# Two-layer streaming trunk on one core: squares behind two z products, token blocks in pairs, z between halves of q, k, v, swapped queries copied on ScalarE

## The chip, the core and the metric

The kernel runs on one core of a Trainium2 chip. The core has TensorE (matrix products; PE in the profile, its weight loads PEld), VectorE (DVE), ScalarE (ACT), GpSimd (POOL) and SyncE (SP, which here issues nearly all the DMAs). Each engine runs its own list of instructions in order and waits on semaphores for the others. The metric is the device time of one execution in microseconds; the time of a kernel is the median of its runs.

## The reference

The input x has 2048 tokens of 1024 channels. Layer A is a gated pooling mixer, layer B stick-breaking attention; both end in a gated embedding add.

```python
def pool_mixer(h, w_in, w_group, scale, w_out):
    u, z = jnp.split(h @ w_in, 2, axis=-1)
    ...
    mixed = jnp.einsum('bsgc,gcd->bsgd', pooled, w_group).reshape(B, S, D_MODEL) * scale
    return (mixed * jax.nn.silu(z)) @ w_out

def reference(x, p, ...):
    for i in range(DEPTH):                     # 2 layers
        if i < N_A:
            h = rms_norm(x, a_norm[i])
            x = x + pool_mixer(h, a_w_in[i], a_w_group[i], a_scale[i], a_w_out[i])
        else:
            kv_in = rms_norm(x, kv_norm)
            k_all, v_all = jnp.split(kv_in @ w_kv, 2, axis=-1)
            k_sh = rms_norm(split_heads(k_all), k_norm)
            v_sh = split_heads(v_all)
            h = rms_norm(x, b_norm[j])
            q, z = jnp.split(h @ b_w_in[j], 2, axis=-1)
            q = rms_norm(split_heads(q), b_q_norm[j])
            o = stick_breaking_attention(q, k_sh, v_sh)   # 16 heads of 64
            x = x + (o * jax.nn.silu(z)) @ b_w_out[j]
        x = x + (p[i] @ ple_w[i]) * jax.nn.sigmoid(x @ ple_gate_w[i])
    return x
```

All of it is float32. The kernel keeps that precision by splitting an operand into a high and a low part, so that one product takes three matmuls (high x high, high x low, low x high).

## The kernel before

**Tiles.** Tokens are cut into four chunks of 512 (`s` or `c`). Activations are held as 8 tiles of 128 channels x 512 tokens, each a pair (high, low): `xp` is the input, `mp` the mixer's result, `x1` and `x2` the stream after the mixer and after layer A. Weights come in units of 512 KB, the buffers `wpair`, nine in all (`UNITS`). A product of z, of the gate or of an output takes a unit for two tiles of input channels; a unit of q, k or v (`plan_wide`) holds one tile of input channels (`kt` 0 to 7) for 512 output columns. The list `plan` sets the order in which units are loaded. `take` hands them out, `give_back` releases one behind its last matmul and lets the next load start.

A unit that is seen for the first time is loaded raw (`wraw`, 256 KB) and split by ScalarE (L176) and VectorE (L177); most are also stored split (`once`), and later chunks load the 512 KB from there. The q, k, v weights come in two halves of eight heads (`b` 0 and 1). The second half is stored in chunk 1 only, so chunks 0 and 1 both split it.

**The stream.** All dense work is one generator, `stream`. For each chunk `first_part` runs the mixer, the output product, the gate and the embedding product, then z of layer B (`gate_z`) and q, k, v of half 0; `second_part` runs q, k, v of half 1. In chunk 3 z stands behind q, k, v of half 0. Behind the last chunk comes `post`, the end of layer B for each chunk.

**q, k and v.** `kvq` computes one of them for one half: four token blocks `j` of 128 tokens, each over eight `kt`: 32 steps of three matmuls (`psd<-wpair,x` in the profile). The list `STEPS` is the order of the steps: token block 0, then 1, then 2 and 3 overlapped. A unit is given back behind its step with `j == 3`. A finished block goes from PSUM through ScalarE: `keyed` normalises rows of q and k per head, `valued` takes v. The rows of q and k are transposed (`finish`, queued in `lag`) at fixed steps of the following block, those of (1, 2), (1, 6), (2, 2), (3, 1). The token norm `r2` is made once per chunk, by whoever needs it first.

**Attention.** It starts when q, k, v of half 0 of chunk 0 are done. From there on TensorE's order is fixed by program order: `front` (logits of 128 queries with 512 keys), `turn` (transposes of the weights), `gather` (products with the values), and between them `fill` takes a set number of steps of the stream, more in early chunks and fewer in late ones. For each head, `load_q` fetches the query tile `qa` (two parts of 64 rows) and `qb`, the same with its parts swapped; both multiply the key tile.

**The start.** Before the attention `dense` takes banks of three tags and a scheduler may move instructions. At the very start (`boot`, `mixer_first`) the weights of the pooled branch are folded, and the first chunk's tokens are squared on ScalarE (L417) and summed by TensorE with narrow 128x1 matmuls (`square_first`), between the matmuls of the second z product. `norm_first` makes of it the norm that the mixer waits for.

Of the kernel before, what the change touches and what calls it, by code (L numbers as in the profile page):

```python
# [19 lines left out]
KT = D // P  # L20
NH = 16
HD = 64
W5 = 512
WB = 256
NSUB = S // W5
# [7 lines left out]
def f(ap):  # L33
    return ap.bitcast(F32)
# [3 lines left out]
def trunk_kernel(ctx, tc, x, p, a_norm, wu_t, wz_a, w_group, a_scale, a_w_out, kv_norm, w_kv,  # L38
                 k_norm, b_norm, b_w_q, b_w_z, b_q_norm, b_w_out, ple_a, ple_b, gate_a, gate_b, out):
    nc = tc.nc  # L40
    V, A, G = nc.vector, nc.scalar, nc.gpsimd
# [202 lines left out]
    for s in range(NSUB):  # L244
        for g in (3, 2, 1, 0):
            if s == 0:
                plan_group(g)
            plan_block("za", wz_a, g, g_a, True)
            plan_block("wf", None, g)
        for b in range(4):  # L250
            plan_block("ao", a_w_out, b, keep=True, order=PAIRS[::-1])
        for b in range(4):
            plan_block("ag", gate_a, b, keep=True)
            plan_block("al", ple_a, b, keep=True, order=PAIRS[:1])
        if s + 1 == NSUB:
            plan_kvq(s, 0)
        for b in range(4):
            plan_block("zb", b_w_z, b, g_b, True)
        if s + 1 < NSUB:
            plan_kvq(s, 0)  # L260
        plan_kvq(s, 1)
        if s == 0:
            first_chunk = len(plan)
# [149 lines left out]
    def square_first(i):  # L413
# [4 lines left out]
        for j in range(4):  # L418
            T.matmul(chunk[0]["sums"][:, 0, j : j + 1], sq[:, j * P : (j + 1) * P], ones,
                     start=(i + j == 0), stop=(i == KT - 1 and j == 3))  # L420

    def norm_first():
        chunk[0]["rb1"] = bcast(rooted(chunk[0].pop("sums"), "x"), "x")

    def warm():
        ps = bank("pso", "warm")
# [86 lines left out]
    def mixer_first():  # L513
        ck = chunk[0]
        ck["m"] = {}
        us = take(4)
        pss = [dense(), dense()]
        yield from product(pss[0], us, ck["x"], 0, 0)
        hooks = {3 * i: [lambda i=i: square_first(i)] for i in range(KT)}
        yield from hooked(product(pss[1], us, ck["x"], P, 1), hooks)  # L520
        while later:
            later.pop(0)()
        us = take(4)
        zs = []
        hooks = {8: [norm_first], 9: [lambda: zs.extend(silu(ps, ck["rb1"]) for ps in pss)]}
        for k in range(2):
            ps = dense()
            yield from hooked(product(ps, us, ck["x"], k * P, k), {} if k else hooks)
            pooled(0, 6 + k, ps, zs[k])
        state["boot"] = state["hold"] = False  # L530
        fold_load(2)
        while later:
            later.pop(0)()
# [91 lines left out]

    lag = []

    STEPS = [(j, kt) for j in range(2) for kt in range(KT)]
    STEPS += [(2, 0), (2, 1), (2, 2), (2, 3), (3, 0), (2, 4), (3, 1), (2, 5), (3, 2), (2, 6), (3, 3), (2, 7)]
    STEPS += [(3, kt) for kt in range(4, KT)]  # L630

    def kvq(s, kind, b):
        ck = chunk[s]
        us = take(KT)
        banks = {}
        for j, kt in STEPS:
            tk = slice(j * P, (j + 1) * P)
            if kt == 0:
                banks[j] = dense()
            u = us[kt][0]  # L640
            for xh, wh in ((0, 0), (1, 0), (0, 1)):
                T.matmul(banks[j], ck["x2"][kt][:, xh, tk], u[:, wh, 0], start=(kt == 0 and xh == wh),
                         stop=(kt == KT - 1 and wh == 1))
                if j == 3 and wh:
                    give_back()
                yield
            if lag and (j, kt) in ((1, 2), (1, 6), (2, 2), (3, 1)):
                lag.pop(0)()
            if kt < KT - 1:
                continue  # L650
            if "r2" not in ck:
                ck["r2"] = token_norm(ck["acc2"], "y")
            rj = ck["r2"][:, j : j + 1]
            (valued if kind == "v" else keyed)(s, kind, b, j, banks.pop(j), rj)

    def valued(s, kind, b, j, ps, rj):
        vr = row("vr")
# [124 lines left out]
    def first_part(s):  # L782
        ck = chunk[s]
        yield from mixer(s)
        x1 = yield from out_steps(ck["m"], lambda o: x[o * P : (o + 1) * P, s * W5 : (s + 1) * W5])
        ple = load_ple(0, s)
        yield from gate_steps(x1, ple, put_x2(s))
        ck["side"] = prep(s + 1) if s + 1 < NSUB else iter(())
        if s + 1 < NSUB:
            yield from every(gate_z(s), 48, ck["side"])  # L790
        for kind in "qkv":
            yield from every(kvq(s, kind, 0), 48, ck["side"])
        after(60, lambda: marks.add((s, 0)))
        if s + 1 == NSUB:
            yield from gate_z(s)

    def second_part(s):
        ck = chunk[s]
# [55 lines left out]
    def load_q(c, h):  # L854
        qa, qb = qryt("qa"), qryt("qb")
        nc.sync.dma_start(out=f(qa), in_=qd[c][h].rearrange("l d n -> (l d) n"))
        for l in range(2):
            nc.sync.dma_start(out=f(qb)[(1 - l) * HD : (2 - l) * HD], in_=qd[c][h][l])
        return qa, qb

    def load_k(kc, h):
        kk = keyt("kk")
# [17 lines left out]
    def front(st, j):  # L880
# [1 line left out]
        r0 = W5 - w  # L882
        ps = bank("psl", "psl")
        qs = slice(j * P, (j + 1) * P)
        (qa, qb), kk = st["q"], st["k"]
# [202 lines left out]
```

## Time and profile before

| | |
|---|---|
| Runs (us) | 2770.01, 2779.59, 2778.19 |
| Median (us) | 2778.19 |
| Profiled execution, its own time (us) | 2769.64 |
| Its span (us) | 2767.9 |
| Mean granted TensorE clock | 0.991 |
| DMA | 684.27 MB, mean 247 GB/s |

Stages of the profiled execution, by the matmuls on TensorE: the first z products and squares 13 to 50 us; the q, k, v stages 289 to 445 us (chunk 0, both halves, the start of the attention at 384 among them), 711 to 893 (chunk 1), 1215 to 1428 (chunk 2), 1751 to 1871 and 1948 to 2074 (chunk 3, with z between). A busy TensorE is not one at its peak, as ends of matmuls are modelled; what counts here is idle time between them and the granted clock.

### The profile page before, as it was taken

The page shows a single profiled execution, that of the slowest core. Times are in us where ns is not written, and L with a number is a line of the kernel's source. Part 1 is how long each engine was busy: PE and PEld are TensorE (multiplying, and loading weights), DVE is VectorE, ACT ScalarE, POOL GpSimd, SP SyncE. Part 2 cuts the span into 40 slices and gives each one's busy share as a digit, 9 for nine tenths or more (in the row PEclk, how much of TensorE's full clock was granted, in tenths as well). Part 3 has the DMA queues.
Part 4 walks back from the last instruction along what each step waited for, and adds up shares of the span by engine and source line. Part 5 has one row for each costly group of instructions (what it writes and reads, how often), then busy time and mean ns, then how long its engine had stood idle before and what let it go on. Part 6 is the DMA issues. An engine that isn't in the chain of part 4 may idle for free.

```text
span 2767.9 us, 37889 instructions
## 1 busy us (share of the span) xinstructions
PE 2719.8 (98%) x13406; PEld 2243.3 (81%) x13406; DVE 1811.1 (65%) x2367; ACT 1229.2 (44%) x2412; POOL 759.0 (27%) x617
## 2 busy tenths in 40 slices
PE   9999989999999999999999999999999999999999
PEld 7878868888877888887778888888888888888887
DVE  5636445644445776655558878776787887887842
ACT  4435543233444334454444445554555444445431
POOL 1345432224432332354223212212211201111101
PEclk8999999999999999999999999999999999999999
DMA  6779888687789878877897676778577765766655
GB/s 223 259 279 346 302 245 279 223 270 246 251 289 321 289 256 272 289 263 249 275 304 235 218 228 208 250 219 265 176 244 239 240 205 184 250 209 211 223 170 184
DMA packets 311306, 684.27 MB, mean 247 GB/s; under 512 B 49222, under 2 KB 81990, under 8 KB 311116
## 3 DMA queue, kind: packets, MB, share of 16 engines
q1 hardware_dynamic: 310540, 681.05, 73.9%
q8 instruction: 106, 1.74, 0.3%
q10 hardware_dynamic: 576, 0.79, 0.1%
q14 instruction: 84, 0.69, 0.1%
HBM read 493.45 MB, written 179.90 MB: 243 GB/s over the span
## 4 chain that ended last, share of the span: by engine, by line
PE 86%; DMA 8%; DVE 2%; ACT 1%; POOL 1%; SPq 1%; issue 1%; ACTq 0%; DVEq 0%; POOLq 0%
PE psd L47 59%; PE psl L47 9%; PE pso L47 9%; PE psa L51 8%; DMA wpair<-once 3%; DMA wraw<-in_w_kv_dram 1%; DMA wraw<-in_b_w_q_dram 1%; PE pst L51 1%; DMA vs<-vr 1%; PE pst L47 1%; DMA kd<-hl 0%; DMA wraw<-in_gate_a_dram 0%; ACT wpair L176 0%; DVE wpair L177 0%; DMA xin<-in_x_dram 0%
## 5 line engine op out<-in xcount | busy, mean ns | idle before, releaser
L893 DVE TENSOR_TENSOR_SCAN pp<-pp,floor 128x512 f32<-128x512 f32 (+3 forms) x640 | 772.9, 1208 | 28.9 <-ACT pp L889 26.9
L910 DVE TENSOR_TENSOR at<-psa,at 128x512 fp32r<-128x512 f32 (+3 forms) x640 | 387.6, 606 | 432.6 <-ACT at L908 429.9
L908 ACT CAST at<-psa 128x512 fp32r<-128x512 f32 (+3 forms) x640 | 333.3, 521 | 726.8 <-PE psa L51 706.1
L47 PE MATMUL psd<-wpair,x 128*128 128x512 f32 x2304 | 615.2, 401 | 25.4 <-DMA wpair<-once 12.8
L47 PE MATMUL psd<-x,wpair 128*128 128x512 f32 x2304 | 606.5, 394 | 1.8 <-ACT x L157 1.6
L47 PEld LDWEIGHTS psd<-wpair,x 128*128 128x128 f32 x2304 | 425.2, 190 | 121.3 <-DMA wpair<-once 20.3
L47 PEld LDWEIGHTS psd<-x,wpair 128*128 128x128 f32 x2304 | 427.1, 188 | 90.0 <-ACT x L157 2.0
L47 PE MATMUL psd<-xp,wpair 128*128 128x512 f32 x1536 | 395.5, 398 | 0.4 <-DVE wpair L177 0.2
L47 PE MATMUL pso<-at,vv 128*128 128x512 f32 (+3 forms) x1280 | 360.9, 363 | 0.0
L889 ACT ACTIVATE pp<-psl 128x512 f32<-128x512 f32 (+3 forms) x640 | 344.6, 538 | 8.7 <-PE psl L47 4.4
L51 PE MATMUL psa<-ident,pp 128*128 128x128 f32 x2176 | 343.7, 273 | 3.0 <-DVE at L910 1.5
L51 PEld LDWEIGHTS psa<-ident,pp 128*128 128x128 f32 x2176 | 275.2, 140 | 84.7 <-DVE pp L893 2.3
L47 PEld LDWEIGHTS psd<-xp,wpair 128*128 128x128 f32 x1536 | 286.9, 191 | 59.6 <-DVE wpair L177 1.2
L47 PE MATMUL psl<-kk,qa 128*128 128x512 f32 (+3 forms) x640 | 283.7, 443 | 0.0
L47 PEld LDWEIGHTS pso<-at,vv 128*128 128x128 f32 x1280 | 240.3, 188 | 53.6
L47 PE MATMUL psl<-kk,qb 128*128 128x512 f32 (+3 forms) x640 | 233.8, 365 | 0.0
L47 PE MATMUL psd<-og,wpair 128*128 128x512 f32 x744 | 208.9, 394 | 0.0
L47 PE MATMUL psd<-mp,wpair 128*128 128x512 f32 x768 | 193.0, 392 | 0.0
L47 PEld LDWEIGHTS psd<-mp,wpair 128*128 128x128 f32 x768 | 142.5, 188 | 29.3
L47 PEld LDWEIGHTS psd<-og,wpair 128*128 128x128 f32 x744 | 137.6, 188 | 28.7
L610 POOL TENSOR_TENSOR xj<-x 128x512 f32<-128x512 f32 x64 | 106.2, 1665 | 149.1 <-DVE sg L621 144.8
L158 POOL TENSOR_TENSOR x<-xr,x 128x512 fp32r<-128x512 f32 x32 | 43.1, 1349 | 329.6 <-ACT x L157 297.1
(118 smaller groups left out, 2655.6 us busy)
## 6 DMA issues: line engine op xcount, KB each, us to landing
wpair<-once SPq DMA_DIRECT2D x468, 512.0 KB
once<-wpair SPq DMA_DIRECT2D x116, 512.0 KB
kk<-kd SPq DMA_DIRECT2D x160, 256.0 KB
vv<-vd SPq DMA_DIRECT2D x160, 256.0 KB
wpair<-wf SPq DMA_DIRECT2D x48, 512.0 KB
once<-kp SPq DMA_DIRECT2D x36, 512.0 KB
qd<-hl SPq DMA_DIRECT2D x64, 256.0 KB
qa<-qd SPq DMA_DIRECT2D x64, 256.0 KB
```

Source lines behind the costliest of these rows:

```text
L47: return held_in_order(nc.tensor.matmul(*a, **k))
L51: return held_in_order(nc.tensor.transpose(*a, **k))
L158: lo.tensor_tensor(out=pr[:, 1], in0=src, in1=f(pr[:, 0]), op=ALU.subtract)
L610: G.tensor_tensor(out=xj, in0=f(x1[o][:, 0]), in1=f(x1[o][:, 1]), op=ALU.add)
L889: A.activation(out=pp[:, r0:], in_=ps[:, :w], func=AF.Sigmoid, scale=-1.0)
L893: V.tensor_tensor_scan(out=pp[:, r0:][:, ::-1], data0=pp[:, r0:][:, ::-1], data1=least, initial=1.0 if st["diag"] else st["carry"][j], op0 ...
L908: A.copy(out=at[:, 0, cs], in_=pt[:, cs])
L910: return lambda: V.tensor_tensor(out=at[:, 1, cs], in0=pt[:, cs], in1=f(at[:, 0, cs]), op=ALU.subtract)
```

## The change

Four things are changed.

1. The first squares. The eight rounds of squares stood in the second z product of the first group, from its first matmul on. Three of them now stand behind its matmuls 16, 19 and 22, five in the first product of the pooled branch that follows. `norm_first` is cut in two: the root (`root_first`) behind the last round, the broadcast nine matmuls later.
2. `STEPS`. Token blocks advance in pairs, 0 with 1 and 2 with 3: four steps of the first, then its last four alternating with the first four of the second, then the rest of the second. As the norm `r2` may not be there for q of half 0, the first two blocks are copied raw to SBUF and scaled when the norm is made behind the second.
3. Chunks 1 and 2 take z between the halves of q, k and v, as chunk 3 did; the plan of weight loads follows. Chunk 0 keeps z first.
4. `load_q` loads only `qa`. Two ScalarE copies of 64x512 make `qb` from it, after 14 steps of the stream, or at the first use at the latest. The attention's first front comes 44 steps of the stream behind its first loads, where it was 24.

```diff
-        if s + 1 == NSUB:
+        if s:
             plan_kvq(s, 0)
         for b in range(4):
             plan_block("zb", b_w_z, b, g_b, True)
-        if s + 1 < NSUB:
+        if not s:
             plan_kvq(s, 0)
...
+    def root_first():
+        chunk[0]["r1"] = rooted(chunk[0].pop("sums"), "x")
+
     def norm_first():
-        chunk[0]["rb1"] = bcast(rooted(chunk[0].pop("sums"), "x"), "x")
+        chunk[0]["rb1"] = bcast(chunk[0].pop("r1"), "x")
...
-        hooks = {3 * i: [lambda i=i: square_first(i)] for i in range(KT)}
+        hooks = {15 + 3 * i: [lambda i=i: square_first(i)] for i in range(3)}
         yield from hooked(product(pss[1], us, ck["x"], P, 1), hooks)
-        while later:
-            later.pop(0)()
         us = take(4)
         zs = []
-        hooks = {8: [norm_first], 9: [lambda: zs.extend(silu(ps, ck["rb1"]) for ps in pss)]}
+        hooks = {3 * i: [lambda i=i: square_first(3 + i)] for i in range(5)}
+        hooks[12] += [root_first] + later
+        later.clear()
+        hooks |= {21: [norm_first], 22: [lambda: zs.extend(silu(ps, ck["rb1"]) for ps in pss)]}
...
-    STEPS = [(j, kt) for j in range(2) for kt in range(KT)]
-    STEPS += [(2, 0), (2, 1), (2, 2), (2, 3), (3, 0), (2, 4), (3, 1), (2, 5), (3, 2), (2, 6), (3, 3), (2, 7)]
-    STEPS += [(3, kt) for kt in range(4, KT)]
+    STEPS = []
+    for j in (0, 2):
+        STEPS += [(j, kt) for kt in range(4)]
+        STEPS += [(j + i, kt + 4 * (1 - i)) for kt in range(4) for i in (1, 0)]
+        STEPS += [(j + 1, kt) for kt in range(4, KT)]
...
+            done = [(j, banks.pop(j))]
             if "r2" not in ck:
+                qs = row("qs")
+                A.copy(out=qs, in_=done[0][1])
+                early.append((j, qs))
+                if j == 0:
+                    continue
                 ck["r2"] = token_norm(ck["acc2"], "y")
-            rj = ck["r2"][:, j : j + 1]
-            (valued if kind == "v" else keyed)(s, kind, b, j, banks.pop(j), rj)
+                done = early
+            for i, ps in done:
+                rj = ck["r2"][:, i : i + 1]
+                (valued if kind == "v" else keyed)(s, kind, b, i, ps, rj)
...
-        if s + 1 < NSUB:
+        if not s:
             yield from every(gate_z(s), 48, ck["side"])
         for kind in "qkv":
             yield from every(kvq(s, kind, 0), 48, ck["side"])
         after(60, lambda: marks.add((s, 0)))
-        if s + 1 == NSUB:
-            yield from gate_z(s)
+        if s:
+            yield from every(gate_z(s), 48, ck["side"])
...
-        for l in range(2):
-            nc.sync.dma_start(out=f(qb)[(1 - l) * HD : (2 - l) * HD], in_=qd[c][h][l])
-        return qa, qb
+        left = [0, 1]
+
+        def swap():
+            while left:
+                l = left.pop()
+                A.copy(out=qb[(1 - l) * HD : (2 - l) * HD], in_=qa[l * HD : (l + 1) * HD])
+
+        after(14, swap)
+        return qa, qb, swap
...
-    for _ in range(24):
+    for _ in range(44):
```

How the built order changes, at three places. First, TensorE at the start: the row with `uh` and `ul` is the folding of weights, `xp` the z products, `sq` the first square.

```order
 L47 MATMUL psd<-wpair,ul 128x256
 L47 MATMUL psd<-wpair,uh 128x256
-L47 MATMUL psd<-xp,wpair 128x512 x25
+L47 MATMUL psd<-xp,wpair 128x512 x40
 L47 MATMUL pst<-ones,sq 128x1 x4
 L47 MATMUL psd<-xp,wpair 128x512 x3
```

The first round of squares moves 15 wide matmuls back; behind it the rounds still alternate with three wide ones each.

Second, TensorE in k of half 0 of chunk 1, from its fourth step on. Before (here `psd_7024` is the bank of token block 0, `psd_7076` that of block 1, and a number of `wpair` is a weight unit, `wpair_6767` the first and `wpair_6998` the last of eight):

```order
L47 MATMUL psd_7024<-wpair_6941,x2_6022 128x512 x3
L47 MATMUL psd_7024<-wpair_6967,x2_6084 128x512 x3
L47 MATMUL psd_7024<-wpair_6986,x2_6156 128x512 x3
L47 MATMUL psd_7024<-wpair_6991,x2_6224 128x512 x2
L47 MATMUL pso_6924<-at_6895,vv_6361 128x256 x2
L47 MATMUL psd_7024<-wpair_6991,x2_6224 128x512
L47 MATMUL psd_7024<-wpair_6998,x2_6308 128x512 x3
L47 MATMUL psd_7076<-wpair_6767,x2_5861 128x512 x3
L47 MATMUL psd_7076<-wpair_6922,x2_5882 128x512 x3
```

The same place of the change (`psd_6555` is block 0, `psd_6582` block 1, `wpair_6289` the first unit, `wpair_6529` the last; `pst` are the transposes of q's rows):

```order
L47 MATMUL psd_6555<-wpair_6488,x2_6006 128x512 x3
L47 MATMUL psd_6582<-wpair_6289,x2_5835 128x512 x3
L47 MATMUL psd_6555<-wpair_6496,x2_6067 128x512 x3
L47 MATMUL pso_6449<-at_6381,vv_5895 128x256 x2
L47 MATMUL psd_6582<-wpair_6456,x2_5867 128x512 x3
L47 MATMUL psd_6555<-wpair_6515,x2_6153 128x512 x3
L47 MATMUL psd_6582<-wpair_6464,x2_5931 128x512 x3
L51 MATMUL pst_6600<-ident_60,qs_6413 128x128
L51 MATMUL pst_6600<-ident_60,qs_6424 128x128
L51 MATMUL pst_6600<-ident_60,qs_6501 128x128
L51 MATMUL pst_6600<-ident_60,qs_6544 128x128
L47 MATMUL psd_6555<-wpair_6524,x2_6218 128x512 x3
```

Units 4 to 7 stood in consecutive steps and now stand in every second one; the transposes of the block before move from behind the eleventh step to behind the ninth.

Third, ScalarE in chunk 0's attention, around the last front of one head (`pp`, 128x512) and the first of the next (`pp`, 128x128). Before:

```order
L908 CAST at_4628<-psa_4625 128x256
L889 ACTIVATE pp_4635<-psl_4632 128x512
L157 CAST mp_4592<-us_4582 128x512
L908 CAST at_4688<-psa_4686 128x128
L889 ACTIVATE pp_4701<-psl_4698 128x128
```

The change, at the same place:

```order
L929 CAST at_4665<-psa_4662 128x256
L910 ACTIVATE pp_4672<-psl_4669 128x512
L876 COPY qb_4724<-qa_4723 64x512 x2
L157 CAST mp_4639<-us_4629 128x512
L480 ACTIVATE sg_4686<-zr_4685 128x512
L929 CAST at_4720<-psa_4718 128x128
L910 ACTIVATE pp_4731<-psl_4728 128x128
```

The two copies for the head after next stand directly behind the `pp` of the front whose query buffers their load takes over.

More of the change, by code (lines that the diff above doesn't have):

```diff
@@ L634, in kvq @@
         us = take(KT)
-        banks = {}
+        banks, early = {}, []
         for j, kt in STEPS:
@@ L884, in front @@
         qs = slice(j * P, (j + 1) * P)
-        (qa, qb), kk = st["q"], st["k"]
+        (qa, qb, swap), kk = st["q"], st["k"]
+        swap()
         T.matmul(ps[:, :w], qa[:, qs], kk[:, :w], start=True, stop=False)
```

## The prediction

> **What bounds the kernel now.** I read the page first, then busy time by stage, then what TensorE waited for, then its timeline at the places where it waited. The page's first lines:
>
> ```profile
> span 2767.9 us, 37889 instructions
> PE 2719.8 (98%) x13406; PEld 2243.3 (81%) x13406; DVE 1811.1 (65%) x2367; ACT 1229.2 (44%) x2412; POOL 759.0 (27%) x617
> ...
> L47 PE MATMUL psd<-wpair,x 128*128 128x512 f32 x2304 | 615.2, 401 | 25.4 <-DMA wpair<-once 12.8
> L47 PE MATMUL psd<-x,wpair 128*128 128x512 f32 x2304 | 606.5, 394 | 1.8 <-ACT x L157 1.6
> ```
>
> TensorE is busy 98% of the span, so only time in which it stood still or ran at a lower clock can be won. The two groups are equal in count and shape. The first is q, k and v, the second z and the gate products: q, k, v alone carry 25.4 us of idle. Now by stage (columns: stretch in us, its length, busy time of TensorE, its weight loads, VectorE, ScalarE and GpSimd, granted clock, DMA share, GB/s):
>
> ```profile
> 20.60:25.80 5.20, 2.56 (x20) 2.37 (x20) 2.21 (x6) 4.90 (x11) 0.00 (x0) 1.00 1.02 407
> 25.80:43.70 17.90, 17.90 (x68) 16.16 (x68) 5.23 (x10) 6.15 (x13) 0.00 (x0) 0.50 0.67 236
> 43.70:49.70 6.00, 6.00 (x18) 4.94 (x19) 0.89 (x2) 1.07 (x3) 1.24 (x2) 0.50 0.80 268
> ...
> 289.40:445.50 156.10, 148.21 (x680) 119.73 (x679) 75.70 (x108) 76.92 (x126) 57.48 (x52) 0.99 0.81 259
> 711.50:893.20 181.70, 169.87 (x809) 137.29 (x808) 92.01 (x132) 85.50 (x163) 60.93 (x53) 0.97 0.84 281
> 1215.30:1427.70 212.40, 200.39 (x978) 162.65 (x977) 118.77 (x155) 97.58 (x191) 71.28 (x60) 0.98 0.79 261
> 1751.30:1870.70 119.40, 119.40 (x627) 99.04 (x626) 87.02 (x111) 61.41 (x119) 25.32 (x23) 1.00 0.73 239
> 1870.70:1947.80 77.10, 75.65 (x385) 62.36 (x384) 51.76 (x63) 34.29 (x70) 16.91 (x11) 1.00 0.79 249
> ...
> 445.50:711.50 266.00, 266.00 (x1267) 221.41 (x1266) 133.90 (x185) 83.58 (x178) 86.54 (x77) 1.00 0.80 260
> ```
>
> The loss sits in four places. At the first squares TensorE stands 5.20 - 2.56 = 2.6 us and then runs 17.9 + 6.0 = 23.9 us at half clock, which wastes 12.0: 14.6 us. The q, k, v stages of token chunks 0, 1 and 2 lose 7.9 + 11.8 + 12.0 = 31.7 us idle, and (1 - clock) x length, 1.6 + 5.5 + 4.2 = 11.3 us, to a lower clock: 43 us. A stage of other products (the last row) loses nothing. Chunk 3, which has z between its halves already, loses nothing before z and 1.5 us in it. The whole ceiling is 58 us.
>
> **Squares (boot).** The timeline of TensorE, then of ScalarE, at the first squares (start, length, what, count, idle before):
>
> ```profile
> 23.29 1.05 PE L47 MATMUL pst<-ones,sq 128*128 128x1 f32 x8 [2.64 <-ACT sq L417]
> 24.20 0.95 PE L47 MATMUL psd<-xp,wpair 128*128 128x512 f32 x3
> 24.99 0.95 PE L47 MATMUL pst<-ones,sq 128*128 128x1 f32 x8
> 25.81 1.63 PE L47 MATMUL psd<-xp,wpair 128*128 128x512 f32 x3
> ...
> 28.80 1.63 PE L47 MATMUL psd<-xp,wpair 128*128 128x512 f32 x3
> ...
> 64.12 21.95 PE L47 MATMUL psd<-xp,wpair 128*128 128x512 f32 x96
> ```
>
> ```profile
> 22.61 4.25 ACT L417 ACTIVATE sq<-xin 128x512 f32<-128x512 f32 x8
> ```
>
> A wide matmul at full clock takes 21.95 / 96 = 0.23 us. Today the first square is wanted after 25 wide matmuls, at 20.65; ScalarE starts it at 22.61. After the change it is wanted after 40, that is 15 x 0.23 = 3.4 us later, at 24.1. ScalarE's new order puts two weight splits (about 0.9 us) ahead of the first square, so it ends near 24: the 2.6 us go, give or take 0.3.
>
> The question is the clock. A round of squares (4 narrow matmuls, 8 records) with its three wide ones took 25.81 - 24.20 = 1.61 us warm, and 28.80 - 25.81 = 2.99 us at half clock. Three stretches of 3.41 us, the length of the short clock drops, each ending where the clock may change:
>
> ```profile
> 22.39:25.80 3.41, 2.51 (x19) 2.37 (x20) 0.96 (x3) 3.41 (x8) 0.00 (x0) 1.00 1.04 417
> 1251.18:1254.59 3.41, 1.74 (x8) 1.08 (x6) 1.82 (x2) 0.00 (x0) 1.11 (x1) 1.00 1.02 399
> ...
> 1285.32:1288.73 3.41, 1.31 (x6) 0.72 (x5) 0.50 (x1) 0.00 (x0) 0.00 (x0) 1.00 1.03 412
> ```
>
> The clock fell behind the first and the third stretch, not behind the second. So 1.74 us of wide work (51%) keeps it and 1.31 (38%) does not. The first looks busiest, with 2.51, but 0.8 of that is wide work and the rest squares: squares hardly count as work. After the change rounds follow each other unbroken, and wide work is 0.69 to 0.79 of 1.61 us, 43 to 49%, inside the gap between 38 and 51%. I take it that the clock still falls, one or two such stretches into the rounds, near 29 us: three rounds are warm, five cold (5 x 1.38 = 6.9 us lost), and the wide work behind them runs cold for some 5 us more (2.6 lost). That leaves 12.0 - 9.5 = 2.5 us won on the clock, with the wait 5; since the fall may come later, I take **6 us**. Ends: 2.6 (only the wait goes) and 14.6 (no fall).
>
> The Trainium skill (TensorE: Matmul & The Clock Gate, "The HAM clock gate") has the clock halve only after an idle window of about 3.4 us; by it no fall would come in the rounds, and the sum would be 8.6 us lower. The first of the three rows speaks against it: only 0.9 us of that stretch was idle.
>
> **Pairs, and z between the halves.** TensorE's waits in all, and its timeline where they are longest in chunk 1 (v half 0, q half 1, k half 1):
>
> ```profile
> PE psd L47 <- DMA wpair<-once: 12.8, 13, 2.1
> PE psd L47 <- ACT wpair L176: 11.4, 6, 3.3
> PE pst L51 <- DVE hl L158: 2.7, 1, 2.7
> ```
>
> ```profile
> 767.33 0.96 PE L47 MATMUL psd<-wpair,x 128*128 128x512 f32 x3 [0.31 <-DMA wpair<-once]
> 769.26 0.97 PE L47 MATMUL psd<-wpair,x 128*128 128x512 f32 x3 [0.97 <-DMA wpair<-once]
> 771.20 0.97 PE L47 MATMUL psd<-wpair,x 128*128 128x512 f32 x3 [0.97 <-DMA wpair<-once]
> ...
> 806.05 3.65 PE L47 MATMUL psd<-wpair,x 128*128 128x512 f32 x9 [3.32 <-ACT wpair L176]
> ...
> 834.60 1.58 PE L47 MATMUL psd<-wpair,x 128*128 128x512 f32 x3 [1.67 <-ACT wpair L176]
> 838.55 3.26 PE L47 MATMUL psd<-wpair,x 128*128 128x512 f32 x7 [2.37 <-ACT wpair L176]
> ```
>
> Every wait falls in a block's first eight steps (a step is one weight unit for one token block, three matmuls), at units 3 to 7: a block wants eight new units in its first eight steps, while the block before gives them back one in two steps, and late. With pairs, units 4, 5, 6, 7 are wanted 1, 2, 3, 4 steps later; units 0 to 3 as before. A step in chunk 1 lasts (181.7 - 11.8 - 5.5) / 192 = 0.86 us, so those units gain 0.9 to 3.4 us; in chunk 0, (156.1 - 9.5) / 192 = 0.76, in chunk 2, (212.4 - 16.2) / 192 = 1.0 a step. Chunk 1: v half 0 is late by 3.4 us in total, of which the wait at unit 3 stays, about 1; q half 1 comes behind z, which wants a unit every two steps, and loses its 3.3; k half 1 is late by 4.0 at unit 7 against 3.4 gained: 0.6 stays. No wait is then long enough for a clock drop. Chunk 1 keeps about 3 of 17.3. Chunk 2, worked alike, keeps about 5 of 16.2 (its first units, and half of the 2.7 us behind VectorE, which pairs don't touch). Chunk 0, whose order of stages stays, keeps 6 of 9.5, as two of its waits are at unit 3 and for a norm. Won: 14 + 11 + 3 = **28 us**, and 2 less, 26, since a step that no longer waits wants the next block's units sooner. Ends: 10 (waits move to the later units) and 43.
>
> What is late next is the transpose of the finished rows. It stands in the next block ahead of the eleventh step, and now ahead of the ninth: two steps, 1.5 to 2 us, sooner. Rows of k come late, and I estimate **4 us** in all; ends 0 and two steps for each of the six blocks behind k in chunks 0 to 2, 11. The two raw copies and the sums of squares at q's start stand after 16 steps, 48 matmuls, as the sums behind z's first two products do today, where TensorE did not wait: 0.
>
> **Swapped queries.** Each head loses two loads of 128 KB and gains two ScalarE copies of 64x512. The nearest rows: the same copy out of PSUM, and how long 256 KB took to land in the chain.
>
> ```profile
> L925 ACT COPY os<-pso 64x512 f32<-64x512 f32 x64 | 37.2, 582 | 42.2 <-PE pso L47 41.5
> ```
>
> ```profile
> 290.81 3.69 DMA xin<-in_x_dram
> 312.50 5.49 DMA xin<-in_x_dram
> ```
>
> 128 x 0.58 = 74 us of ScalarE's time, hidden as long as it has its 56% idle. But in the new order the copies stand right behind the pp of the front that frees the query buffer, so they wait there for a load that starts only then: ScalarE is held some 4 us, once a head. Behind it wait the next pp and at (wanted a front later), weight splits, and the eviction of psd. In q, k, v a bank is wanted again five steps, 3.8 us or more, after it is full: covered. In the gate stage it is wanted after six matmuls, 1.4 us and the attention between: not covered in chunk 1, two or three heads, up to 2 us each. **4 us** lost; ends 0, and 1 us a head, 64. The lighter queue (64 x 256 KB less) I cost at nothing: q, k, v wait for order more than for bytes. The 20 further steps ahead of the first front only move work.
>
> **Sum.** Against the profiled execution's own 2769.6 us (span 2767.9 and 1.7 around it): 2769.6 - 6 - 26 + 4 + 4 = 2745.6. The runs shown have their median 8.6 us above that execution, two of three near 2779; I add a quarter of it, 2, for 2748.
>
> **Rivals.**
> 1. The clock stays up through the squares. For it: 43 to 49% wide work lies inside the gap; against it: squares counted for little. 8.6 us less: 2739.
> 2. Arrival, not order, limits the units: DMA share is 0.84 in chunk 1, and the waits move from steps 3 to 7 to steps 5 to 11. Then 10 us are won, not 26: 2764. Against it: chunk 3 and z lose little at a DMA share of 0.73 to 0.79, though at longer steps.
> 3. The copies hold ScalarE, and TensorE with it. For it: their place. Against it: ScalarE is 44% busy, and at q, k, v's evictions there are five steps. At 1 us a head, 64 us: 2748 - 4 + 64 = 2808. From 0.5 us a head (32 us) the gain is gone.
> 4. The change doesn't do what it says: the scheduler could put rows back. The built order shows 40 wide matmuls ahead of the first square and the pairs interleaved, so only its smallest part, chunk 0's, could be lost: 2751, inside the forecast.
>
> **How the numbers follow.** Forecast (with 4) 0.45, rival 1 0.28, rival 2 0.19, rival 3 0.08. Range: low from rival 1 with half of the 17 us left in q, k, v gone too and none of the holding cost, 2739 - 8 - 8 = 2723, set at 2722; high from rival 2 with the transposes at their end, 2764 + 7 = 2771, and the runs' own scatter, set at 2776. Half a per cent of the median is 13.9 us, about what a measurement of this kernel can tell from no change: faster means under 2764.3, slower over 2792. The forecast and rival 1 are faster, and so are four in ten of rival 2: 0.79. Most of rival 2's rest and a third of rival 3 are the same: 0.15. Slower: 0.06.
>
> **What would show it.** The idle of 2.6 us at the first square gone, and a half-clock stretch that begins near 29 us and ends near 44 to 48 (right), or none (rival 1). Idle in q, k, v of chunk 1 down from 11.8 to about 3 us with the clock at 1.00; no wait in q half 1; the rest at unit 3, or waits before steps 7 to 11 (rival 2). Waits of the transposes for VectorE's qs of some us. ScalarE waiting for the qa load about 64 times; TensorE waiting for ScalarE's sg in the gate stage of chunk 1. The prediction is wrong if weight units come no sooner with fewer bytes queued, or if ScalarE's held time reaches TensorE.

## The result, and the profile after

| | before | the change |
|---|---|---|
| Runs (us) | 2770.01 to 2779.59 (4 runs) | 2747.89, 2742.08, 2746.70, 2747.56 |
| Median (us) | 2776.39 | 2747.13 |
| Profiled execution, its own time (us) | 2769.64 | 2747.89 |
| Its span (us) | 2767.9 | 2746.1 |

The ratio of the change to the kernel before is 0.9894, 95% interval 0.9871 to 0.9916: about 29 us are won, and 2748.0 was forecast. The sum came out, but not its terms. The spans differ by 21.8 us, less than the medians, as the profiled execution of the kernel before is a little faster than the four runs, and that of the change is the slowest of its four; the account that follows is of that difference.

The page of the change:

```profile
span 2746.1 us, 37869 instructions
PE 2703.7 (98%) x13406; PEld 2232.5 (81%) x13406; DVE 1803.7 (66%) x2367; ACT 1302.9 (47%) x2542; POOL 763.6 (28%) x617
...
L47 PE MATMUL psd<-wpair,x 128*128 128x512 f32 x2304 | 604.2, 398 | 9.3 <-ACT qs L703 5.4
L47 PE MATMUL psd<-x,wpair 128*128 128x512 f32 x2304 | 606.1, 394 | 4.7 <-ACT sg L621 2.7
```

The idle of the q, k, v matmuls (first group) fell from 25.4 to 9.3 us, and what ended it is no longer a weight unit but ScalarE's `qs`. The z and gate products (second group) went from 1.8 to 4.7, now behind ScalarE's `sg`. ScalarE itself is 74 us busier, as 128 copies of 0.58 had it.

Busy time by stage of the change: the rounds of squares; q, k, v of chunk 0; of chunk 1, half 0 and half 1; of chunk 2, the same two; and two pieces at half clock, one inside chunk 0 and one right behind chunk 2 (columns as in the prediction: stretch, length, busy PE, weight loads, VectorE, ScalarE, GpSimd, granted clock, DMA share, GB/s):

```profile
23.55:35.60 12.05, 12.05 (x86) 11.10 (x86) 4.28 (x10) 7.21 (x15) 0.00 (x0) 1.00 1.03 403
...
276.80:434.70 157.90, 148.06 (x674) 119.66 (x673) 76.57 (x107) 79.60 (x129) 60.52 (x52) 0.97 0.78 249
651.40:734.50 83.10, 81.56 (x404) 67.15 (x402) 34.53 (x51) 43.09 (x85) 42.99 (x37) 1.00 0.75 241
786.30:867.90 81.60, 81.45 (x404) 67.59 (x403) 49.04 (x72) 46.33 (x86) 26.10 (x23) 1.00 0.83 296
1129.30:1230.00 100.70, 97.15 (x494) 80.12 (x492) 59.55 (x75) 56.29 (x113) 50.17 (x40) 1.00 0.73 248
1293.10:1392.10 99.00, 96.08 (x485) 78.98 (x483) 58.28 (x75) 47.42 (x92) 27.13 (x26) 1.00 0.77 258
...
378.73:388.97 10.24, 5.93 (x14) 4.67 (x15) 5.74 (x9) 4.55 (x8) 5.36 (x4) 0.50 0.77 254
...
1392.49:1395.90 3.41, 3.41 (x11) 2.73 (x10) 3.41 (x5) 2.46 (x5) 0.00 (x0) 0.50 1.09 352
```

The prediction read a stage as idle = length - busy, and loss to the clock = (1 - clock) x length. That counts idle time at half clock once more, and the clock column has two digits only. In chunk 1 of the kernel before, TensorE was busy for 3.41 + 4.46 = 7.9 us of the 10.2 us at half clock:

```profile
807.45:810.86 3.41, 3.41 (x13) 2.82 (x12) 1.29 (x2) 2.03 (x4) 1.61 (x2) 0.50 0.85 311
834.76:841.59 6.83, 4.46 (x10) 2.88 (x11) 2.07 (x3) 2.57 (x4) 0.00 (x0) 0.50 1.03 413
```

So the loss to the clock is taken here as half of the busy time at half clock. For the kernel before that gives 9.6 us lost in chunk 0 (the prediction has 9.5), 11.8 + 3.9 = 15.8 in chunk 1 (17.3) and 12.0 + 5.1 = 17.1 in chunk 2 (16.2). In the change the rounds of squares lose nothing. Chunk 1 loses 1.5 + 0.2 = 1.7 us. Chunk 2 loses 3.6 + 2.9 = 6.5, and 1.7 more in the half-clock stretch behind it. Chunk 0 loses 9.8 + 3.0 = 12.8. Of that, 7.8 belong to one place: a wait of 4.83 us, and 10.24 us at half clock, which began 0.5 us into the wait and so lie over it for 4.3 us.

What TensorE waited for, in the whole of the change (us, times, longest):

```profile
PE psd L47 <- ACT qs L703: 5.4, 2, 4.8
PE psa L51 <- DVE pp L914: 4.8, 4, 2.5
PE psa L51 <- DVE at L931: 4.1, 5, 1.8
PE psd L47 <- ACT sg L621: 2.7, 2, 1.9
PE psd L47 <- ACT vr L672: 2.6, 2, 2.4
PE psa L51 <- DVE hl L158: 2.3, 1, 2.3
PE psd L47 <- DMA wpair<-once: 2.1, 2, 1.3
...
PE pst L51 <- DVE qs L710: 1.8, 2, 1.2
PE pst L51 <- DVE at L931: 1.5, 2, 1.1
...
PE psd L47 <- ACT wpair L176: 1.2, 2, 0.8
```

The two rows for weight units, 12.8 and 11.4 us before, are down to 2.1 and 1.2. New are the rows with `qs` and `vr` on ScalarE, the evictions of banks of q, k and v: 4.8 us in chunk 0 and 2.4 at the end of chunk 2. Grown are the rows with `pp` and `at`: the attention's own transposes (`psa`) and what is queued behind them wait for VectorE, 4.8 + 4.1 + 1.5 = 10.4 us, nearly all of it after 1400 us. Before, these two and the wait for `qs` were:

```profile
PE pst L51 <- DVE qs L696: 1.9, 2, 1.6
...
PE psa L51 <- DVE at L910: 1.5, 1, 1.5
PE psa L51 <- DVE pp L893: 1.3, 2, 0.9
```

| where the span's 21.8 us come from | us |
|---|---|
| squares: the matmul behind the first mixer starts at 170.27, was 184.50 | -14.2 |
| q, k, v of chunk 1 (1.7 lost for 15.8) | -14.1 |
| q, k, v of chunk 2 (6.5 for 17.1) | -10.6 |
| the half-clock stretch behind chunk 2, at 1392 | +1.7 |
| q, k, v of chunk 0 (12.8 for 9.6) | +3.2 |
| gate of chunk 0 (idle time and half clock, 5.9 for 4.6) | +1.3 |
| gates of chunks 1 and 2, waits for sg | +2.7 |
| attention, waits for pp and at (10.4 for 2.8) | +7.6 |
| a half-clock stretch of 3.4 us behind the longest of these, at 1860 | +1.7 |
| sum | -20.7 |

So 38.9 us were won and 18.2 given back, where the prediction had 32 won and 8 given back.

### The profile page after: what moved, and what is told of

Same layout as the page of the kernel before. It is cut to its first block, busy times and chain, and to the rows that moved or that the text cites. A ratio compares the mean times of both kernels' runs of the same rounds, so it can differ in the third digit from the quotient of the medians.

```text
span 2746.1 us, 37869 instructions
## 1 busy us (share of the span) xinstructions
PE 2703.7 (98%) x13406; PEld 2232.5 (81%) x13406; DVE 1803.7 (66%) x2367; ACT 1302.9 (47%) x2542; POOL 763.6 (28%) x617
## 4 chain that ended last, share of the span: by engine, by line
PE 86%; DMA 6%; DVE 3%; ACT 2%; issue 1%; POOL 1%; SPq 1%; ACTq 0%; DVEq 0%; POOLq 0%
PE psd L47 59%; PE psl L47 8%; PE pso L47 8%; PE psa L51 8%; DMA qa<-qd 1%; DMA wraw<-in_w_kv_dram 1%; DVE pp L914 1%; PE pst L51 1%; DMA vs<-vr 1%; DMA xin<-in_x_dram 1%; DMA wpair<-once 0%; DVE at L931 0%; PE pst L47 0%; DMA wraw<-in_gate_a_dram 0%; DMA kd<-hl 0%
## 5 line engine op out<-in xcount | busy, mean ns | idle before, releaser
L914 DVE TENSOR_TENSOR_SCAN pp<-pp,floor 128x512 f32<-128x512 f32 (+3 forms) x640 | 760.6, 1188 | 25.6 <-ACT pp L910 24.1
L47 PE MATMUL psd<-wpair,x 128*128 128x512 f32 x2304 | 604.2, 398 | 9.3 <-ACT qs L703 5.4
L47 PE MATMUL psd<-xp,wpair 128*128 128x512 f32 x1536 | 390.0, 394 | 2.6 <-ACT vr L672 2.4
L955 POOL TENSOR_TENSOR os<-os,zt 128x512 f32<-128x512 f32 x32 | 43.9, 1373 | 339.0 <-ACT os L954 282.8
```

The lines of the kernel that those rows point to most:

```text
L47: return held_in_order(nc.tensor.matmul(*a, **k))
L914: V.tensor_tensor_scan(out=pp[:, r0:][:, ::-1], data0=pp[:, r0:][:, ::-1], data1=least, initial=1.0 if st["diag"] else st["carry"][j], op0 ...
L955: G.tensor_tensor(out=os, in0=os, in1=zt, op=ALU.mult)
```

## The experiments

My theory was this: the squares, the pairs and z's place each win by themselves; the copies of `qb` hold ScalarE and cost some us; chunk 0's long wait is a `qs` eviction queued on ScalarE behind weight splits. Rivals stand with each run. First the four parts, each undone alone.

**Squares back** in the second z product, from its first matmul on:

```diff
-        hooks = {15 + 3 * i: [lambda i=i: square_first(i)] for i in range(3)}
+        hooks = {3 * i: [lambda i=i: square_first(i)] for i in range(KT)}
...
+        hooks = {8: [root_first, norm_first], 9: [lambda: zs.extend(silu(ps, ck["rb1"]) for ps in pss)]}
...
```

> The change with the first squares put back into the second z product (rounds from its first matmul on, root and broadcast together behind the ninth matmul of the product that follows). Theory: the boot's gain came whole, 2.6 us of wait and 12 us of half clock, and is kept to the end, since TensorE sets the end: the profile shows the wait of 2.6 us and some 24 us at half clock again, and the time is 14 to 15 us above the change, about 2761. Rival: what boot won is given back where a later stage waits for DMA; then the time rises by less than 8 us, and a wait of the change gets shorter by the rest.

Measured: 2759.66 us (2757.27 to 2768.03), ratio to the kernel before 0.9954 (0.9941 to 0.9967). TensorE's timeline of this run, at the first squares (start, length, what, count, idle before):

```profile
23.29 1.05 PE L47 MATMUL pst<-ones,sq 128*128 128x1 f32 x8 [2.66 <-ACT sq L417]
...
27.14 1.70 PE L47 MATMUL pst<-ones,sq 128*128 128x1 f32 x8
```

The wait and the fall are back (the squares of a round grow from some 0.95 to 1.70 us), and the matmul behind the mixer starts at 184.50 again. The place of the squares is worth 12.5 us between medians, 14.2 in the traces. (The medians of the change and of these runs come from different chips, on which the kernel before took 2771.5 to 2776.4 us; a difference of one or two us between them says nothing.)

**The old order of steps**, pairs undone:

```diff
+    STEPS = [(j, kt) for j in range(2) for kt in range(KT)]
+    STEPS += [(2, 0), (2, 1), (2, 2), (2, 3), (3, 0), (2, 4), (3, 1), (2, 5), (3, 2), (2, 6), (3, 3), (2, 7)]
+    STEPS += [(3, kt) for kt in range(4, KT)]
...
```

> The change with the old order of steps (token blocks 0, 1, then 2 with 3). Theory: pairs removed the waits at weight units 3 to 7 in chunks 1 and 2 and brought a new wait to chunk 0, where a block's second bank is wanted five steps behind its last use and no longer nine: unit waits come back in v half 0 and k half 1 of chunks 1 and 2, 10 to 14 us with their clock drops, the wait of 4.8 us in chunk 0 for ScalarE's qs and its 10 us at half clock go (10 us won); net 0 to 4 us above the change, 2747 to 2751. Rival 1: z between the halves did the work in chunks 1 and 2; then few waits come back there, and without the bank wait the kernel is 8 to 10 us faster, 2738. Rival 2: pairs did it all, also in chunk 0: 14 us slower or more.

Measured: 2765.61 us (2761.87 to 2767.09), ratio 0.9968 (0.9955 to 0.9980): 18.5 us above the change. That is rival 2 and not the theory, which had at most 4. Its timeline in v of half 0 of chunk 1:

```profile
709.65 0.96 PE L47 MATMUL psd<-wpair,x 128*128 128x512 f32 x3 [0.84 <-DMA wpair<-once]
711.56 0.96 PE L47 MATMUL psd<-wpair,x 128*128 128x512 f32 x3 [0.95 <-DMA wpair<-once]
```

The step-by-step waits are back although z stands between the halves. Chunk 0's wait of 4.8 us for `qs` is gone here, but three waits for weight splits (1.3, 2.1, 2.3) stand in its place, and the stage is no shorter. So the pairs win in chunks 1 and 2, and chunk 0 gains nothing by giving them up.

**z ahead of both halves** in chunks 1 and 2, as before:

```diff
-        if not s:
+        if s + 1 < NSUB:
...
-        if s:
+        if s + 1 == NSUB:
```

> The change with z of chunks 1 and 2 ahead of q, k, v again. Theory: with pairs, only q half 1 and what follows it in a row of six blocks lose: 4 to 8 us of unit waits in half 1 of chunks 1 and 2, 2751 to 2755. Rival: pairs alone are enough, no change (2745 to 2749). Other rival: z in front carried the gain, 15 us or more slower, 2762.

Measured: 2753.20 us (2748.56 to 2759.25), ratio 0.9930 (0.9917 to 0.9944): z's place is worth 6 us between medians. Its trace doesn't show where: the profiled execution is the fastest of the five and its span, 2746.8 us, is only 0.7 above that of the change, though the waits for stored units (3.9 for 2.1) and for VectorE's part of the splits (3.0 for 0.7) are longer.

**qb by DMA again**, the hold of 44 steps kept:

```diff
+        for l in range(2):
+            nc.sync.dma_start(out=f(qb)[(1 - l) * HD : (2 - l) * HD], in_=qd[c][h][l])
+        return qa, qb, lambda: None
...
```

> The change with the swapped queries loaded by DMA again, two loads of 128 KB a head (the 44 steps ahead of the first front stay). Theory: the copies hold ScalarE (it waited 116 us in 53 places for the query load), which costs TensorE the waits for ScalarE's sg in the gate stages (2.7 us) and part of those for pp and at in the attention (8.9 us, 2.9 before): the kernel is 3 to 8 us faster, 2739 to 2744, and ScalarE's waits for qa are gone. Rival: the lighter queue of loads is worth more than the hold costs: unit waits in q, k, v come back and the kernel is 3 us slower or more, 2750 and up.

Measured: 2740.63 us (2737.02 to 2742.26), ratio 0.9877 (0.9864 to 0.9891): 6.5 us below the change. Where the cost comes from shows in the change's timelines in the gate of chunk 1, first ScalarE, then TensorE:

```profile
606.30 0.60 ACT L910 ACTIVATE pp<-psl 128x512 f32<-128x512 f32 x1
609.44 0.62 ACT L876 CAST qb<-qa 64x512 fp32r<-64x512 f32 x1 [2.54 <-DMA qa<-qd]
...
610.73 0.62 ACT L876 CAST qb<-qa 64x512 fp32r<-64x512 f32 x1
611.37 0.60 ACT L621 ACTIVATE sg<-psd 128x512 f32<-128x512 f32 x1
```

```profile
612.02 2.32 PE L47 MATMUL psd<-x,wpair 128*128 128x512 f32 x9 [1.87 <-ACT sg L621]
```

ScalarE stands 2.54 us behind a `pp` until the query tile has landed; `sg`, which empties the bank that the next gate product wants, is queued behind the copies; and TensorE waits 1.87 us for it. With `qb` loaded, the same place runs through:

```profile
610.06 2.21 PE L47 MATMUL psd<-x,wpair 128*128 128x512 f32 x9
```

In the whole of the change ScalarE was held 53 times for that load, 116.1 us in all, but little of it reached TensorE. That the copies cost 6.5 us is measured; where all of it goes is not. With `qb` loaded the span is 5.6 us shorter. The waits for `sg` are still 1.7 us (one, in the gate of chunk 2) and those of the attention 8.6 for 10.4, which makes 2.8; the wait for `vr` is 1.6 shorter, and the two half-clock stretches at 1392 and 1860 are gone, although the wait in front of the second still lasts 2.23 us. Other waits grew.

**The clock and the squares.** Is it the narrow matmuls that let the clock fall? A round behind every single wide matmul, all eight in the second z product from the same place on:

```diff
-        hooks = {15 + 3 * i: [lambda i=i: square_first(i)] for i in range(3)}
+        hooks = {15 + i: [lambda i=i: square_first(i)] for i in range(8)}
```

> The change with a round of squares (four narrow matmuls) behind each single wide matmul instead of behind three: wide work falls from 46% of the rounds' time to about 22%, with no wait of TensorE in front, and the rounds last some 8.4 us, two whole stretches of 3.4 us. Theory: narrow matmuls count little as work, and it is the 46% of wide work that kept the clock up in the change; here the clock falls within the rounds and stays at half for 7 to 14 us: 2750 to 2755. Rival: the clock fell before because of the wait of 2.6 us, and narrow matmuls count as work; then it stays at 1.00 through the rounds and the time is that of the change, 2747.

Measured: 2751.38 us (2747.88 to 2755.85), ratio 0.9917 (0.9903 to 0.9931). Its windows from 23.8 us on:

```profile
23.80:27.20 3.40, 3.40 (x27) 3.15 (x26) 0.60 (x3) 3.40 (x8) 0.00 (x0) 0.94 1.05 424
27.20:30.60 3.40, 3.40 (x15) 3.21 (x16) 1.50 (x4) 1.94 (x5) 0.00 (x0) 0.50 0.97 357
```

The profile shows no idle time of TensorE here, and the clock fell all the same, at 26.8 us, one window into the rounds. Wide work, 0.23 us in a round of 1.13 at full clock, was 20% of the time. So narrow matmuls count for little, as the prediction had it, and a fall needs no idle time that the profile shows. (It models the ends of matmuls, so short gaps between narrow ones would not be seen.) As far as that goes, this is against the Trainium skill (TensorE: Matmul & The Clock Gate, "The HAM clock gate"), which has the clock halve after an idle window.

**The hold of 24 steps** of the stream (one matmul each), else the change:

```diff
-    for _ in range(44):
+    for _ in range(24):
```

> The change with 24 steps of the stream ahead of the first front, as before. The attention's waits for pp and at (8.9 us in the change, 2.9 before) came back in each of the four kernels with one part undone, and the 44 steps stand in all four. Theory 1: the 44 steps set dense work against other fronts, and with 24 those waits fall to about 3 us: 5 us faster, 2742. Theory 2: those waits come from ScalarE's and VectorE's new order by the scheduler and stay: 2745 to 2749. Theory 3: the first front then waits for its key and value tiles at the start of the attention: 2 to 5 us slower.

Measured: 2741.20 us (2740.56 to 2748.37), ratio 0.9888 (0.9875 to 0.9900). The run that was profiled is the highest, and in it the clock fell in the boot, which is built like that of the change:

```profile
24.23 1.05 PE L47 MATMUL pst<-ones,sq 128*128 128x1 f32 x8 [0.25 <-ACT sq L417]
...
27.95 1.70 PE L47 MATMUL pst<-ones,sq 128*128 128x1 f32 x8
```

Only 0.25 us of wait is new. So the rounds of the change lie at the edge: of the ten traces of kernels with these rounds, this is the only one in which the clock fell there.

**Copies on GpSimd, splits on GpSimd.** The first moves the copies of `qb`, the second the high parts of the raw q, k, v weights of half 1, both away from ScalarE:

```diff
-                A.copy(out=qb[(1 - l) * HD : (2 - l) * HD], in_=qa[l * HD : (l + 1) * HD])
+                G.tensor_copy(out=qb[(1 - l) * HD : (2 - l) * HD], in_=qa[l * HD : (l + 1) * HD])
```

```diff
+            if late:
+                G.tensor_scalar(out=pr[:, 0, i], in0=raw[:, i], scalar1=g, scalar2=1.0, op0=ALU.mult, op1=ALU.mult)
+            else:
+                booted(A.activation(out=pr[:, 0, i], in_=raw[:, i], func=AF.Identity, scale=g))
...
```

> The change with the two copies of the swapped queries on GpSimd instead of ScalarE; the queue has as little to load as in the change. Theory: the hold on ScalarE is what the swap costs (loading by DMA again made it 6 us faster), so with it off ScalarE the waits for sg go, 2.7 us, and the time is that of the kernel with loads or lower, 2737 to 2742. Rival 1: the copies are late for their first use wherever they run, or hold GpSimd likewise: 2745 to 2750. Rival 2: GpSimd is slow at such copies and holds the sums of x1, norms and gating behind it: 2755 and more.

> The change with the high parts of the raw weight units of q, k, v of half 1 (split in chunks 0 and 1) made on GpSimd instead of ScalarE. In the change TensorE waits 4.8 us in chunk 0 for ScalarE's eviction of a bank, which stands behind weight splits that wait for their raw loads. Theory: the order on ScalarE makes that wait, so it goes, with most of 10 us at half clock: 5 to 10 us faster, 2738 to 2742. Rival: the raw loads themselves are late, so TensorE waits the same time one unit further, now for wpair: within 3 us of the change.

Measured: 2750.66 us (2739.45 to 2758.26), ratio 0.9913 (0.9897 to 0.9929), and 2747.03 us (2745.04 to 2748.59), ratio 0.9902 (0.9890 to 0.9915). Neither differs from the change by what can be told, so both theories missed. In the first no wait for `sg` is left, but transposes of q's and k's rows wait for VectorE's `qs`, 10.8 us in 7 waits, one of them 4.0. In the second this is chunk 0's place (timeline of TensorE):

```profile
385.28 0.33 PE L51 MATMUL pst<-ident,qs 128*128 128x128 f32 x1 [2.37 <-DVE qs L713]
388.90 0.48 PE L51 MATMUL pst<-ident,qs 128*128 128x128 f32 x1 [3.29 <-DVE qs L713]
```

The 4.8 us for the bank are gone, and 5.7 us for the rows, two steps of the same chain further on, have come. For comparison the change itself, ScalarE and then TensorE:

```profile
379.95 0.72 ACT L176 ACTIVATE wpair<-wraw,gains 128x512 fp32r<-128x512 f32 x1 [1.52 <-DMA wraw<-in_w_kv_dram]
...
381.10 1.32 ACT L176 ACTIVATE wpair<-wraw,gains 128x512 fp32r<-128x512 f32 x2
382.33 0.66 ACT L703 ACTIVATE qs<-psd,r 128x512 f32<-128x512 f32 x1
```

```profile
376.93 1.29 PE L47 MATMUL psd<-wpair,x 128*128 128x512 f32 x3 [0.40 <-ACT wpair L176]
383.04 6.45 PE L47 MATMUL psd<-wpair,x 128*128 128x512 f32 x15 [4.83 <-ACT qs L703]
```

The eviction `qs` stands on ScalarE behind splits that wait for raw weights to land, and TensorE cannot start its next bank until it is done. Taking the splits away shows that they held the eviction, and that something else was due at the same time. The end of chunk 2 in the change is of the same kind, ScalarE and then TensorE:

```profile
1390.85 0.62 ACT L170 CAST kp<-kraw 128x512 fp32r<-128x512 f32 x1 [3.61 <-DMA kd<-hl]
1391.38 0.68 ACT L672 ACTIVATE vr<-psd,r 128x512 f32<-128x512 f32 x1
```

```profile
1392.11 0.50 PE L47 MATMUL psd<-xp,wpair 128*128 128x512 f32 x1 [2.37 <-ACT vr L672]
```

Here v's eviction stands behind a split in front of which ScalarE waits 3.61 us for a DMA. The half-clock stretch at 1392 follows.

**Both repairs together**: `qb` by DMA and the hold of 24; and the same with a round behind every four wide matmuls.

```diff
-        hooks = {15 + 3 * i: [lambda i=i: square_first(i)] for i in range(3)}
+        hooks = {14 + 4 * i: [lambda i=i: square_first(i)] for i in range(3)}
...
-        hooks = {3 * i: [lambda i=i: square_first(3 + i)] for i in range(5)}
-        hooks[12] += [root_first] + later
+        hooks = {4 * i + 2: [lambda i=i: square_first(3 + i)] for i in range(5)}
+        hooks[18] += [root_first] + later
...
```

> The change, but qb is loaded by DMA again (no copies on ScalarE) and the hold is 24 steps again instead of 44. Each alone gave 2740.6 and 2741.2 us, against 2747.1 us for the change. Theory: they pay in different places (the copies in the gate banks that wait for sg and in ScalarE's queue, the hold in the attention's waits for pp and at), so they add: 2747.1 - 6.5 - 5.9 = 2734.7, from 2732 to 2738, in the runs in which the clock stays up in the boot. Rival: both remove the same waits, those of the attention: 2740.6, from 2738.5 to 2743. A run in which the clock falls in the boot stands 7 to 9 us above the others and has a mean clock 0.003 lower, under either.

> As b_swap24, but a round of squares stands behind every four wide matmuls instead of three (from the 14th of the second z product on; the root behind the 18th of the product after it, its transpose behind the 22nd). Wide work is then 53% of the stretch instead of 46%. Theory: the clock falls where wide work is under about half of a window of 3.4 us, and at 46% the rounds lie at the edge, so that the phase decides (it stayed at 1 in the run of the change that was profiled, and fell in one of e_24 with the same rounds): with 53% no run falls, the mean clock is 0.996 or more in each, and the median is that of the undisturbed runs of b_swap24, with up to 1 us more where the root's transpose now waits. Rival: the falls don't hang on the share of wide work: about one run in four or five still stands 7 to 9 us above the rest, at a mean clock of 0.993 or 0.994.

Measured: 2736.94 us (2735.45 to 2743.00), ratio 0.9880 (0.9861 to 0.9899), and 2739.43 us (2735.01 to 2739.97), ratio 0.9880 (0.9865 to 0.9894). On their chip the kernel before took 2771.47 us, 3 to 5 less than beside the other runs. So the first lies where the theory had it in us, but 34.5 us below the kernel before, where either repair alone was 33 to 34 below: that the two add is not shown. Its trace says why it might not. Attention's waits for `pp` and `at` fell to 1.5 us, but rows of q and k are now what is late:

```profile
PE pst L51 <- DVE qs L710: 5.7, 3, 3.8
PE psd L47 <- ACT qs L703: 5.1, 2, 4.2
PE pst L51 <- DVE hl L158: 3.9, 3, 2.5
```

In the second all four runs have a mean clock of 0.996 or 0.997, as the theory wants. But of the 47 runs of kernels with three wide matmuls to a round only seven had 0.994 or less, so four without a fall say little; and the median is 2.5 us higher, where at most 1 was expected. It is no better version.

**The change and the hold of 24 on one chip**, as the hold's cost was read across chips:

> The change itself once more, unedited, so that it stands on one chip beside c_24: the medians so far came from several chips, on which the kernel before took between 2771.5 and 2776.4 us. Theory (the longer hold costs about 6 us): 2745 to 2748 us, some 28 to 30 us below the kernel before of the same chip. Rival (the 6 us are differences of the chips): 2741 to 2743, within 2 us of c_24.

> The change with the hold of 24 steps, as e_24, beside c_again on one chip, and both with the undisturbed clock: runs with a mean clock of 0.994 or less (the clock fell in the boot) are compared apart. Theory (the hold of 44 steps delays the attention's transposes and evictions): 5 to 7 us below c_again. Rival (no difference): within 2 us of it. In between, the hold costs less than e_24 had it look.

Measured: 2746.06 us (2743.10 to 2759.96, 6 runs), ratio 0.9913 (0.9893 to 0.9934), and 2740.48 us (2736.30 to 2747.60, 5 runs), ratio 0.9886 (0.9869 to 0.9903). Two runs of the first, 2759.96 and 2756.67, had a mean clock of 0.991 and 0.993; they have no trace, so that it was the boot is a guess. Without them its median is 2745.1, and the hold costs 4.6 to 5.6 us, at the lower end of what the theory wanted. The waits of the attention, first of the change here, then of the hold of 24:

```profile
PE psa L51 <- DVE pp L914: 4.0, 4, 1.5
PE psa L51 <- DVE at L931: 3.8, 6, 1.8
...
PE pst L51 <- DVE at L931: 2.4, 3, 1.1
```

```profile
PE psa L51 <- DVE at L931: 4.1, 4, 1.8
...
PE psa L51 <- DVE pp L914: 1.0, 2, 0.7
```

10.2 us against 5.1, as 10.4 against 4.7 in the first pair. The wait for `vr`, 2.6 and 2.7 us in the two traces of the change, is in neither trace of the hold of 24; waits for `qs` and `hl` are longer there. That the hold makes the attention's waits is shown; by which step of the interleaving, is not, and it wasn't tried.

## Why the prediction was right, and where it was wrong

**The mechanism of the bound was right.** The time was won where TensorE stood or ran cold, and the edits, each undone alone, nearly add up to it: squares 12.5, pairs 18.5, z 6, copies -6.5 and hold -5 make 25.5 of the 29 us. Each taken against the kernel before on its own chip, they are 14.2, 20.2, 7.8, -4.8 and -5.6 (the hold by the last pair), 31.8 in all.

**Boot, 6 us: mis-sized, 14.2 in the trace.** The wait went as forecast, the first round at 23.55 for 24.1. "I take it that the clock still falls" failed: rival 1 happened, at its upper end. The bracket (38% fell, 51% stayed) was right and 46% lay inside it, and e_24's run shows that it can go the other way; there it fell near 27, for 29 forecast. What the step lacked was any reason to put the edge above 46%.

**Pairs and z, 26 us, with 4 given back by the transposes: right in chunk 1, nearly in chunk 2, wrong in chunk 0.** Chunk 1 won 14.1 (14 forecast, from 17.3 where 15.8 were lost), chunk 2 10.6 less the 1.7 behind it, 8.9 (11), waits of the transposes included; all waits for stored units together are 2.1 us, so rival 2 is out. Chunk 0 was to win 3 and lost 3.2, though its waits for units did fall, from 4.4 to 1.7. The step that failed is "a bank is wanted again five steps, 3.8 us or more, after it is full: covered". With pairs a block's second bank is wanted sooner, and ScalarE was not free for it: in chunk 0 the eviction stood behind three splits and their raw loads, 4.83 us, and with the half clock that lies over and behind that wait the place lost 7.8 us. At the end of chunk 2 it failed again, 2.37 us for `vr` and 1.7 at half clock; without the pairs waits for `vr` are 0.4 us in all (u_pairs), and with the hold of 24 there are none. I had priced that cover by time alone and not by what stands in ScalarE's queue, though the same paragraph named the splits there. The transposes' 4 us did not come: the waits behind `qs` are 1.8 us where they were 1.9, and that behind `hl` 2.3 where it was 2.7.

**Copies of qb, 4 us: right in mechanism where it was looked for, a little small.** The place, the load that holds ScalarE, `sg` in the gate of chunk 1 and the price were as put (2.7 us in the gates); undone, they give 6.5, of which the waits for `sg` and of the attention show 2.8; the rest lies in waits and half-clock stretches further on, and how the copies bring those about is not shown. Rival 3, 1 us a head, is out: 116 us of held ScalarE cost TensorE some 6.

**Hold of 44, "only move work": wrong, about 5 us.** It was costed at nothing without a row; a shift of all the attention against the stream needed a bound on both sides, like any other edit.

So three steps were wrong, by 8 us to the good (boot), 6 to the bad (chunk 0) and 5 to the bad (hold), and the transposes' 4 us, which were not lost, stand against the 2.5 that the copies cost beyond their 4 and the 2 by which chunk 2 fell short. They largely cancelled, and that the predicted time came out within 1 us of the median is in part luck. Two slips of the prediction change nothing in the time: the chance of faster adds up to 0.81, not 0.79, and the transposes stand behind the eleventh and now the ninth step, not ahead of them.

## What to carry to other kernels

Where a block wants all its weight units in a row, let two blocks share the stretch: the later units are wanted later at no cost in matmuls, as long as the emptied banks and the finished rows, which are wanted sooner, do not stand behind waiting work on their engine. An instruction that waits for a DMA should not be put behind the very step that lets that DMA start, on an engine that also empties PSUM. And an offset between two interleaved streams is an edit of its own: undo it alone before saying that it only moves work.

## What was not expected of the hardware

The clock fell without any idle time in front of it that the profile shows, some 3 us into the rounds, when 20% of the time went to wide work (e_dense); at 46% it stayed at 1.00 through all eight rounds in the profiled runs of the change and fell in that of e_24, whose order of TensorE there is the same. A wait of 0.25 us, or where the stretch begins, seems to decide; which of them, the runs don't tell.
